# Tiles in multiples of 256 bytes and a later norm factor in a two-layer decoder trunk

## The chip, the cores and the metric

The kernel runs on one core of a Trainium2 chip. The metric is the device time of one execution in microseconds (us). Each core has a matrix engine (TensorE, "PE" in the profile; its loading of the stationary operand is "PEld"), a vector engine (DVE), a scalar engine (ACT), GpSimd (POOL) and SyncE (SP), which here only issues transfers. The engines run side by side, each through its own queue of instructions in order; 16 DMA engines move data between HBM and SBUF, the on-chip memory of 128 partitions. PE accumulates into PSUM banks.

## The reference

The input `x` is 256 tokens by 2,048 features (S = 256, D = 2048). Two layers follow each other, each with a mixer and a gated MLP, both behind an RMS norm and added to the residual stream.

```python
for l in range(DEPTH):
    h = rms_norm(x, mix_norm[l])
    h = mixer_ab(h, ...) if l % 2 == 0 else mixer_c(h, ...)
    x = x + h
    h = rms_norm(x, ffn_norm[l])
    x = x + conv_ffn(h, ffn_w_up[l], ffn_conv_w[l], ffn_conv_b[l], ffn_w_down[l])

def rms_norm(x, gain):
    return x * rsqrt(mean(x * x, axis=-1) + eps) * gain

def conv_ffn(h, w_up, conv_w, conv_b, w_down):
    z = h @ w_up                      # 2048 -> 2 * 5632
    z = causal width-3 convolution over tokens of z, + conv_b
    a, b = split(z, 2)
    return (silu(a) * b) @ w_down     # 5632 -> 2048
```

Mixer AB (layer 0) is a chunked gMLP with 8 heads beside an HGRN2 recurrence with 8 heads, both fed by one projection 2048 -> 6144, and one output projection 2048 -> 2048. Mixer C (layer 1) is attention with 16 heads, normed q and k, a forget gate and an output gate: 2048 -> 8208, and 2048 -> 2048 back. All is float32.

## The kernel before

**Arithmetic.** Every weight is streamed from HBM once, as float32, in blocks of 128 partitions x 1,024 columns (512 KB). `weights` (L142) allocates three tiles for a block: `w`, filled by a DMA on SP's queue (L150); `wh`, a rounded copy that ACT makes (L153); and `wl`, the remainder `w - wh`, by DVE (L155). Activations are split likewise: each 128-feature slice has a tile `a` (or `ya`, `yb`, `yc`, `hid`) of 512 columns, high part in 0 to 255 and low part in 256 to 511. A product is then three matmuls on PE: high x `wh`, high x `wl`, low x `wh`.

**Three forms of a projection.** `project` keeps features on partitions (L176, L179). `project_tok` (L212 to L214, and L204 for the first four slices of the kernel) has the activations stationary (128 tokens) and 512 columns of weights moving, so that tokens lie on partitions. `project_four` (L229 to L231) does the same with four 128-column pieces of the weights, and runs w_abo, w_co and all of both MLPs: 16 slices of 128 make 8 blocks of 12 matmuls for each group of 512 output columns. Its result, tokens on partitions, goes back to features on partitions in `transposed`: 32x32 transposes on DVE (L237) and 16 DMAs of 32 KB, by turns on SP's and POOL's queue (L242).

**Norm.** The projections run on `x * gain`, not normed. Squares are summed slice by slice into `acc` (ACT L314, DVE L315). `finish_tok` (L322) lets PE sum `acc` over partitions with `ones` (L326), yields once, and `rsq` (L279) makes `Rt`, one factor per token, by Ln and Exp on ACT (L99) and steps on DVE. In the MLP `four` (L771) reads `norm.Rt` right behind its `project_four` and scales the result by it as it leaves PSUM.

**Order.** The program is traced in the order of the Python code. Work beside the matmuls lies in generators: `queue` holds those not begun, `flight` those running; `tick` (L121), called before every block of weights, fills `flight` up to `depth[0]` and advances each one by a step. `LAG` = 4 ticks is the time a generator leaves for transposing DMAs. A scheduler of the framework then orders each engine's queue by the dependencies and the traced order.

**Memory.** Pools give every tag a fixed place in each partition, tag after tag, so the size of a tile sets where the tiles behind it begin. Small tiles (factors, sums) are 16 floats = 64 bytes wide (`LANE` = 16), and `pp`, the table of per-feature constants, 816 floats. The main weight pool `wp` (4 buffers of `w`, 3 each of `wh` and `wl`) exists throughout; the MLPs have a second one, `fw`, with 2 of each, which `weights` uses for every second block from turn 7 of the MLP on:

```python
if deep["pool"] is not None and deep["turn"] > 6 and deep["turn"] % 2:
    pool, nw, ns = deep["pool"], 2, 2
else:
    pool, nw, ns = wp, 4, 3
```

`fw` and the MLP's own pool `fp` lie where the mixer's tiles lay, so the first transfers into them wait until the mixer's last tiles have been read: those are read by `add_four`'s rest (L359), which adds w_co's or w_abo's result to x and feeds the next norm.

**Start.** SP issues the first weights (L81), `pp`, and further weights; ACT issues five transfers of x (L83), then loads a table of activation functions (L131); PE runs 11 small matmuls on `ones` (L134; 22 rows in the trace) while the data arrive.

Of the kernel before, what the change touches and what calls it, by code (L numbers as in the profile page):

```python
# [8 lines left out]
F32 = mybir.dt.float32  # L9
# [16 lines left out]
LAG = 4  # L26
EPS = 1e-6
WARM = 11
FETCH = {4: (8,), 8: (12,)}
LANE = 16  # L30
# [19 lines left out]
def tile_trunk(ctx: ExitStack, tc: tile.TileContext, x, pp_d, cst_d, mlev_d, msk_d,  # L50
# [80 lines left out]
    SC.preload_act_table_set(LNEXP)  # L131
# [10 lines left out]
    def weights(src, n, rows=None, w=None):  # L142
        deep["turn"] += 1
        if deep["pool"] is not None and deep["turn"] > 6 and deep["turn"] % 2:
            pool, nw, ns = deep["pool"], 2, 2
        else:
            pool, nw, ns = wp, 4, 3
        if w is None:
            w = pool.tile([P, n], F32, tag="w", name=nm("w"), bufs=nw)
            deep["dma"] = nc.sync.dma_start(  # L150
                w if rows is None else w.rearrange("p (m c) -> p m c", m=rows), src)
        wh = pool.tile([P, n], F32R, tag="wh", name=nm("wh"), bufs=ns)
        SC.activation(wh, w, AF.Copy)  # L153
# [64 lines left out]
    def project_four(w4, acts, n, k0=0):  # L218
        ps = [pm.tile([P, 512], F32, tag="pm", name=nm("pm")) for _ in range(2)]
        for k in range(0, n, 2):  # L220
# [3 lines left out]
            for T in range(2):  # L224
                for i in range(2):
# [5 lines left out]
                    PE.matmul(ps[T], al, h, start=False, stop=k + i == n - 1)  # L231
# [47 lines left out]
    def rsq(dst, src, n):  # L279
        tag = "sq" if dst.shape[-1] == S else f"rm{len(dst.shape)}{dst.shape[-1]}"  # L280
# [14 lines left out]
    class Norm:  # L295
# [26 lines left out]
        def finish_tok(self):  # L322
            p2 = bank()
            for T in range(2):
                lhs = self.acc[:, T * P:(T + 1) * P] if not self.turn else view(self.acc, T, (2, P))
                PE.matmul(p2[:, 2 * T:2 * T + 2], lhs, ones[:, 0:2], start=True, stop=True)  # L326
            Rt = cp.tile([P, LANE], F32, tag="Rt", name=nm("Rt"), bufs=2)[:, 0:2]
            yield
# [20 lines left out]
    def add_four(q, ps, z, tmp, dst, nxt):  # L349
# [4 lines left out]
        def rest():  # L354
# [8 lines left out]
            if q == 3:  # L363
                yield
                yield from nxt.finish_tok()
# [4 lines left out]
    def mixer_ab(norm):  # L370
# [40 lines left out]
        SC.dma_start(wt[:, 0], spw_d)  # L411
        SC.dma_start(wt[:, 1], spb_d.partition_broadcast(P))
        SC.dma_start(pp[:, C_CW:NPP], pp_d[:, C_CW:NPP])
        msk = hp.tile([P, NL * P], BF16, tag="msk", name="msk")
        kst = hp.tile([P, NL * P], F32, tag="smk", name="kst", bufs=1)
        SC.dma_start(kst, msk_d)
# [4 lines left out]
        ss = hp.tile([P, 4 * NH], F32, tag="ss", name="ss")  # L421
# [37 lines left out]
        gm = hp.tile([P, 4 * NH], F32, tag="gm", name="gm")  # L459
        mx, sm_, lb, omlb = (gm[:, i * NH:(i + 1) * NH] for i in range(4))  # L460
        ge = hp.tile([P, 4 * NH], F32, tag="ge", name="ge")[:, 0:3 * NH]
# [32 lines left out]
        def hgrn(h):  # L494
# [14 lines left out]
            tot = l  # L509
            for li in reversed(range(NL)):  # L510
# [468 lines left out]
```

## Time and profile before

| what | value |
|---|---|
| median of 3 runs | 2356.82 us (2355.55 to 2357.02) |
| the profiled execution: its time, its span | 2357.62 us, 2355.8 us |
| mean granted PE clock | 0.997 |
| PE, PEld, DVE, ACT, POOL busy | 2340.0, 1931.0, 1583.3, 1291.8, 260.1 us |
| HBM read, mean rate | 435.24 MB, 186 GB/s |
| L229 to L231: on `a`, on `hid` | 3 x 1408, 3 x 688 matmuls |
| L212 to L214 | 3 x 504 matmuls |
| PE idle longest | 1.5 us for wh, 1.3 us for w, 1.2 us for wl, twice 1.0 us for acc |

The table is read so: the span goes from the first to the last instruction on the core, and the time of the execution has 1.8 us around it. A busy time is the sum of an engine's instructions with overlaps counted once; two matmuls that follow each other overlap (one takes 0.39 us from start to end, the next starts 0.23 us behind it), so the distance of their starts, not their duration, is what one costs. Behind a bracket in an answer on groups stand the busy time, the mean duration in ns, and the idle time of the engine ahead of the group. In a timeline the columns are start, duration, engine, line, operation, what is written and read, and in square brackets the idle time before it and what ended it. The clock is the share of full speed that the throttle granted to PE.

### The profile page before, as it was taken

The numbers are of one execution on the slowest core, as the hardware profiler recorded it, in microseconds if no ns is written. First come the engines' busy times: TensorE is split into PE (matmuls) and PEld (weight loads), VectorE is DVE, ScalarE is ACT, GpSimd is POOL, SyncE is SP. The second block draws the span as 40 slices with busy tenths as digits, with TensorE's granted clock in tenths as the row PEclk, the third lists the DMA queues.
The fourth block names the chain that finished last, engine by engine and source line by source line (L and its number), as shares of the span: only waits on it lengthen the run. The fifth ranks groups of instructions, "written<-read, shape, count | busy, mean of one in ns | idle before, by whom it ended". The sixth has DMA issues, their size and how long they took to land.

```text
span 2355.8 us, 31594 instructions
## 1 busy us (share of the span) xinstructions
PE 2340.0 (99%) x10776; PEld 1931.0 (82%) x10776; DVE 1583.3 (67%) x2470; ACT 1291.8 (55%) x1955; POOL 260.1 (11%) x484
## 2 busy tenths in 40 slices
PE   9999999999999999999999999999999999999999
PEld 7888888788888888888788888887888888888887
DVE  7777877666566656766866666766666466557666
ACT  7655665555455545654554455555555455455542
POOL 0000002122012002111100000012121022012102
PEclk9999999999999999999999999999999999999999
DMA  8655567776666767765665555667777667667765
GB/s 269 183 166 153 150 206 219 227 213 204 209 205 198 221 193 205 222 214 177 210 191 180 172 162 165 191 201 226 220 212 216 190 210 214 200 201 215 215 204 166
DMA packets 433009, 470.94 MB, mean 200 GB/s; under 512 B 90688, under 2 KB 394064, under 8 KB 432720
## 3 DMA queue, kind: packets, MB, share of 16 engines
q1 hardware_dynamic: 415904, 449.96, 62.3%
q0 software_dynamic: 15360, 15.76, 3.1%
q10 hardware_dynamic: 1584, 3.21, 0.4%
q8 instruction: 84, 1.38, 0.3%
q14 instruction: 77, 0.63, 0.1%
HBM read 435.24 MB, written 2.11 MB: 186 GB/s over the span
## 4 chain that ended last, share of the span: by engine, by line
PE 95%; DMA 1%; DVE 1%; SPq 1%; issue 1%; ACT 0%; POOL 0%; DVEq 0%; ACTq 0%; POOLq 0%
PE pm L230 22%; PE pm L231 22%; PE pm L229 22%; PE pm L176 8%; PE pm L213 5%; PE pm L214 5%; PE pm L212 5%; PE pm L179 4%; SPq L242 1%; PE px L532 1%; DMA w<-in_w_up 0%; DMA x<-in_x 0%; PE px L713 0%; ACT wh L153 0%; PE px L677 0%
## 5 line engine op out<-in xcount | busy, mean ns | idle before, releaser
L155 DVE TENSOR_TENSOR wl<-w,wh 128x1024 fp32r<-128x1024 f32 (+1 forms) x820 | 998.7, 1221 | 663.0 <-ACT wh L153 655.9
L153 ACT ACTIVATE wh<-w 128x1024 fp32r<-128x1024 f32 (+1 forms) x820 | 864.5, 1056 | 832.7 <-PE pm L231 555.9
L229 PE MATMUL pm<-wh,a 128*128 128x512 f32 x1408 | 553.4, 393 | 2.8 <-ACT wh L153 1.5
L230 PE MATMUL pm<-wl,a 128*128 128x512 f32 x1408 | 553.9, 393 | 0.6 <-DVE wl L155 0.5
L231 PE MATMUL pm<-wh,a 128*128 128x512 f32 x1408 | 554.2, 394 | 0.0
L242 POOL DMA_DIRECT2D zt<-tmp x416 | 225.1, 549 | 1237.3 <-DVE tmp L237 1150.5
L229 PEld LDWEIGHTS pm<-wh,a 128*128 128x128 f32 x1408 | 265.1, 188 | 62.8 <-ACT wh L153 3.0
L230 PEld LDWEIGHTS pm<-wl,a 128*128 128x128 f32 x1408 | 265.4, 188 | 62.2 <-DVE wl L155 1.7
L231 PEld LDWEIGHTS pm<-wh,a 128*128 128x128 f32 x1408 | 265.2, 188 | 59.8
L231 PE MATMUL pm<-wh,hid 128*128 128x512 f32 x688 | 270.0, 392 | 0.0
L230 PE MATMUL pm<-wl,hid 128*128 128x512 f32 x688 | 269.7, 392 | 0.0
L229 PE MATMUL pm<-wh,hid 128*128 128x512 f32 x688 | 269.7, 392 | 0.0
L176 PE MATMUL pm<-a,wh 128*128 128x512 f32 x784 | 251.0, 400 | 0.0
L212 PE MATMUL pm<-wh,a 128*128 128x512 f32 x504 | 200.1, 398 | 0.3 <-ACT wh L153 0.3
L213 PE MATMUL pm<-wl,a 128*128 128x512 f32 x504 | 197.4, 392 | 2.2 <-DVE wl L155 2.2
L214 PE MATMUL pm<-wh,a 128*128 128x512 f32 x504 | 197.0, 391 | 0.0
L179 PEld LDWEIGHTS pm<-a,wl 128*128 128x128 f32 x784 | 147.3, 188 | 34.2
L179 PE MATMUL pm<-a,wl 128*128 128x256 f32 x784 | 155.1, 279 | 0.0
L230 PEld LDWEIGHTS pm<-wl,hid 128*128 128x128 f32 x688 | 129.1, 188 | 29.4
L229 PEld LDWEIGHTS pm<-wh,hid 128*128 128x128 f32 x688 | 129.2, 188 | 29.1
L231 PEld LDWEIGHTS pm<-wh,hid 128*128 128x128 f32 x688 | 129.1, 188 | 29.2
L176 PEld LDWEIGHTS pm<-a,wh 128*128 128x128 f32 x784 | 120.5, 189 | 0.4
(217 smaller groups left out, 2163.5 us busy)
## 6 DMA issues: line engine op xcount, KB each, us to landing
w<-in_w_up SPq DMA_DIRECT2D x352, 512.0 KB, 4.5
w<-in_w_dn SPq DMA_DIRECT2D x176, 512.0 KB, 4.3
w<-in_w_cqkv SPq DMA_DIRECT2D x96, 512.0 KB, 3.8
w<-in_w_abo SPq DMA_DIRECT2D x32, 512.0 KB, 4.5
w<-in_w_cg SPq DMA_DIRECT2D x32, 512.0 KB, 4.4
w<-in_w_co SPq DMA_DIRECT2D x32, 512.0 KB, 4.3
zt<-tmp SPq DMA_DIRECT2D x416, 32.0 KB, 2.5
zt<-tmp POOLq DMA_DIRECT2D x416, 32.0 KB, 2.4
```

The source lines that it names most:

```text
L153: SC.activation(wh, w, AF.Copy)
L155: V.tensor_tensor(wl, w, wh.bitcast(F32), ALU.subtract)
L176: PE.matmul(ps, wh[:, k * P:(k + 1) * P], acts[done + k], start=done + k == 0, stop=False, skip_group_check=True)
L179: PE.matmul(ps[:, S:2 * S], wl[:, k * P:(k + 1) * P], acts[done + k][:, 0:S], start=False, stop=done + k == nk - 1, skip_group_check=True)
L212: PE.matmul(ps[T], ah, h, start=k + i == 0, stop=False)
L213: PE.matmul(ps[T], ah, l, start=False, stop=False)
L214: PE.matmul(ps[T], al, h, start=False, stop=k + i == KT - 1)
L229: PE.matmul(ps[T], ah, h, start=k + i == 0, stop=False)
L230: PE.matmul(ps[T], ah, l, start=False, stop=False)
L231: PE.matmul(ps[T], al, h, start=False, stop=k + i == n - 1)
L242: (nc.sync, nc.gpsimd)[(a + b) % 2].dma_start(dst[BLK * b:BLK * (b + 1), :, a * n:(a + 1) * n], tmp[BLK * a:BLK * (a + 1), b * 4 * n:(b + ...
L532: PE.matmul(sps[:, (li - c0) * P:(li - c0 + 1) * P], E[:, li, 0], E[:, li, 1], start=True, stop=True)
```

## The change

It has four parts.

1. **Sizes.** `LANE` goes from 16 to 64, so small tiles are 256 bytes wide; `ss`, `gm`, `ct` and the tile for `rsq` become 64 floats wide, `ge` moves into `gm`, and HGRN's running products share one tile `tots`. Every SBUF tile is then a multiple of 256 bytes.
2. **The MLPs' norm factor.** `finish_tok` yields twice between L342 (L326 before) and `rsq`, is reached `WAIT` = 4 ticks later, and its matmul is ordered behind the latest matmul of `project_four`. `four` no longer scales its result at once: it returns a generator, `empty`, that yields until `norm.Rt` exists, then moves the result out of PSUM, transposes it, and waits `LAG` ticks; `start` takes a step of it at once and puts it into `flight`. `z` has 2 buffers instead of 3, and the second weight pool serves from turn 13 on.
3. **Mixer C.** The projections of q and k of the first four heads both come before the drain and the norm's end; the projection of the forget gate (`forget`) comes behind them.
4. **Start.** `pp` and the first slice of x are issued by ACT, the next four by POOL, the weights by SP. The first four slices' weights come in tiles of 1,024 columns, loaded and split in halves. The early table load at L131 is left out, 9 warming matmuls replace 11, x from slice 8 on is issued behind another block of weights, and the squares as well as the late constants are ordered behind the ACT copy of turn 5.

The diff, cut to its core:

```diff
@@ -24,10 +24,11 @@
 LAG = 4
+WAIT = 4
 EPS = 1e-6
-WARM = 11
-FETCH = {4: (8,), 8: (12,)}
-LANE = 16
+WARM = 9
+FETCH = {6: (8,), 8: (12,)}
+LANE = 64
 LEVELS = (64, 32, 16, 8, 4, 2, 1)
@@ -77,11 +78,9 @@
-    first = wp.tile([P, 512], F32, tag="w", name=nm("w"), bufs=4)
-    nc.sync.dma_start(first, w_v[0, :, 0:512])
-    for t, c0, n in xload[:5]:
-        SC.dma_start(t, x[:, c0:c0 + n, :])
-    nc.sync.dma_start(pp[:, 0:C_FFN], pp_d[:, 0:C_FFN])
+    SC.dma_start(pp[:, 0:C_FFN], pp_d[:, 0:C_FFN])
+    for i, (t, c0, n) in enumerate(xload[:5]):
+        (nc.gpsimd if i else SC).dma_start(t, x[:, c0:c0 + n, :])
     V.memset(ones, 1.0)
@@ -128,7 +127,11 @@
-    SC.preload_act_table_set(LNEXP)
+    def start(g):
+
+        if next(g, g) is not g:
+            flight.append(g)
+
     warm = pm.tile([P, 512], F32, tag="pm", name="warm")
@@ -139,20 +142,27 @@
-    def weights(src, n, rows=None, w=None):
+    def weights(src, n, rows=None, single=None):
...
-        if deep["pool"] is not None and deep["turn"] > 6 and deep["turn"] % 2:
+        if deep["pool"] is not None and deep["turn"] > 12 and deep["turn"] % 2:
...
-        if w is None:
-            w = pool.tile([P, n], F32, tag="w", name=nm("w"), bufs=nw)
+        w = pool.tile([P, n], F32, tag="w", name=nm("w"), bufs=nw)
+        wh = pool.tile([P, n], F32R, tag="wh", name=nm("wh"), bufs=ns)
+        wl = pool.tile([P, n], F32R, tag="wl", name=nm("wl"), bufs=ns)
+        parts = [slice(i, i + n // 2) for i in (0, n // 2)] if single else [slice(0, n)]
+        for p in parts:
...
-                w if rows is None else w.rearrange("p (m c) -> p m c", m=rows), src)
-        wh = pool.tile([P, n], F32R, tag="wh", name=nm("wh"), bufs=ns)
-        SC.activation(wh, w, AF.Copy)
-        wl = pool.tile([P, n], F32R, tag="wl", name=nm("wl"), bufs=ns)
-        V.tensor_tensor(wl, w, wh.bitcast(F32), ALU.subtract)
+                w[:, p] if rows is None else w.rearrange("p (m c) -> p m c", m=rows), src[:, p] if single else src)
+        for i, p in enumerate(parts):
+            if single:
+                norm, k = single
+                norm.feed_split(k + i, SC if k + i else V)
+            deep["act"] = SC.activation(wh[:, p], w[:, p], AF.Copy)
+            if deep["turn"] == 5:
+                deep["hold"] = deep["act"]
+            V.tensor_tensor(wl[:, p], w[:, p], wh[:, p].bitcast(F32), ALU.subtract)
@@ -184,24 +194,27 @@
-        for c in ((1, 1, 1, 1) + (2,) * 6 if feed else (2,) * 8):
+        for c in (2,) * 8:
...
-                for i in range(c):
-                    norm.feed_split(k + i, V if k == 0 else SC)
+                if k >= 4:
+                    for i in range(c):
+                        norm.feed_split(k + i)
...
-            wh, wl = weights(wsrc[:, k * 512:(k + c) * 512], c * 512, w=first if feed and k == 0 else None)
+            wh, wl = weights(wsrc[:, k * 512:(k + c) * 512], c * 512, single=(norm, k) if feed and k < 4 else None)
...
-            if feed and c == 1:
-                a = norm.a[k]
-                for j, (o, t) in enumerate(((0, wh), (S, wh), (0, wl))):
-                    for T in range(2):
-                        PE.matmul(ps[T], a[:, o + T * P:o + (T + 1) * P], t, start=k + j == 0, stop=False)
+            if feed and k < 4:
+                for i in range(c):
+                    a = norm.a[k + i]
+                    for j, (o, t) in enumerate(((0, wh), (S, wh), (0, wl))):
+                        for T in range(2):
+                            PE.matmul(ps[T], a[:, o + T * P:o + (T + 1) * P], t[:, i * 512:(i + 1) * 512],
+                                      start=k + i + j == 0, stop=False)
@@ -228,7 +241,7 @@
                     PE.matmul(ps[T], ah, l, start=False, stop=False)
-                    PE.matmul(ps[T], al, h, start=False, stop=k + i == n - 1)
+                    deep['mm'] = PE.matmul(ps[T], al, h, start=False, stop=k + i == n - 1)
         return ps
@@ -277,7 +290,7 @@
     def rsq(dst, src, n):
-        tag = "sq" if dst.shape[-1] == S else f"rm{len(dst.shape)}{dst.shape[-1]}"
+        tag = "sq" if dst.shape[-1] == S else "rm"
         cols = dst.shape[-1] if dst.shape[-1] == S else LANE // math.prod(dst.shape[1:-1])
@@ -308,10 +321,13 @@
             if self.n == 0:
-                SC.activation(self.acc, xT[k], AF.Square)
+                r = SC.activation(self.acc, xT[k], AF.Square)
             else:
                 sq = tp.tile([P, S], F32, tag="sq", name=nm("sq"))
-                SC.activation(sq, xT[k], AF.Square)
+                r = SC.activation(sq, xT[k], AF.Square)
+            if "mm" not in deep:
+                tc.add_manual_dep(r.ins, deep["hold"].ins.name, order, reason="not before")
+            if self.n:
                 (eng or V).tensor_tensor(self.acc, self.acc, sq, ALU.add)
@@ -323,8 +339,11 @@
                 lhs = self.acc[:, T * P:(T + 1) * P] if not self.turn else view(self.acc, T, (2, P))
-                PE.matmul(p2[:, 2 * T:2 * T + 2], lhs, ones[:, 0:2], start=True, stop=True)
+                r = PE.matmul(p2[:, 2 * T:2 * T + 2], lhs, ones[:, 0:2], start=True, stop=True)
+                if "mm" in deep:
+                    tc.add_manual_dep(r.ins, deep["mm"].ins.name, order, reason="not before")
             Rt = cp.tile([P, LANE], F32, tag="Rt", name=nm("Rt"), bufs=2)[:, 0:2]
+            yield
             yield
@@ -405,20 +425,24 @@
-        SC.dma_start(cst, cst_d)
-        SC.dma_start(pp[:, C_FFN:C_CW], pp_d[:, C_FFN:C_CW])
+        def fetch_late(*args):
+            r = SC.dma_start(*args)
+            tc.add_manual_dep(r.ins, deep["hold"].ins.name, order, reason="queue order")
+
+        fetch_late(cst, cst_d)
...
@@ -507,6 +531,7 @@
             tot = l
+            tots = hp.tile([P, S], F32, tag="tot", name=nm("tot"), bufs=1)
             for li in reversed(range(NL)):
@@ -518,7 +543,7 @@
                     V.tensor_tensor(odd, odd, view(tot, m, (-m, 2), (2, m // 2), (0, n)), ALU.mult)
-                    nt = hp.tile([P, max(m, LANE)], F32, tag=f"tot{n}", name=nm("tot"), bufs=1)[:, 0:m]
+                    nt = tots[:, S - 2 * m:S - m]
                     V.tensor_tensor(nt, view(tot, 0, (2, m)), view(tot, 1, (2, m)), ALU.mult)
@@ -637,7 +662,7 @@
         A = norm.a
-        early = project_tok(w_cqkv[0], norm)
+        early = project_tok(w_cqkv[0], norm), project_tok(w_cqkv[CH // 4], norm)
         drain()
@@ -648,26 +673,28 @@
-        f = project_norm(w_cf, A, R, hp.tile([P, S], F32, tag="f", name="f"))
...
-        nc.sync.dma_start(cb, cd.partition_broadcast(P))
+        ct = hp.tile([P, 2, 2 * CH], F32, tag="ct", name="ct")[..., 0:CH]
+
+        def forget():
+            f = project_norm(w_cf, A, R, hp.tile([P, S], F32, tag="f", name="f"))
+            fa = hp.tile([P, S], F32, tag="fa", name="fa")
...
+            V.tensor_tensor_scan(fc, on, f, 0.0, ALU.mult, ALU.add)
+            cd = dp.tile([CH, S], F32, tag="cd", name="cd")
+            nc.sync.dma_start(cd, fc[0:CH, :])
+            for T in range(2):
+                ps = bank()
+                PE.transpose(ps[:, 0:P], fc[:, T * P:(T + 1) * P], ident)
+                V.tensor_copy(ct[:, T], ps[:, 0:CH])
+            nc.sync.dma_start(cb, cd.partition_broadcast(P))
@@ -716,9 +743,11 @@
             qkv = []
-            ss = hp.tile([P, 2, 2, 4], F32, tag="ss", name=nm("ss"), bufs=2)
+            ss = hp.tile([P, 2, 2, LANE // 4], F32, tag="ss", name=nm("ss"), bufs=2)[..., 0:4]
             for j in range(3):
-                ps = early if g + j == 0 else project_tok(w_cqkv[j * (CH // 4) + g], norm)
+                if g == 0 and j == 2:
+                    forget()
+                ps = early[j] if g == 0 and j < 2 else project_tok(w_cqkv[j * (CH // 4) + g], norm)
                 z = hp.tile([P, 2, 512], F32, tag=f"z{j}", name=nm("z"), bufs=2)
@@ -770,13 +799,19 @@
             ps = project_four(w_up[l, j0:j0 + 4], A, KT)
-            Rt = norm.Rt
             tmp, zt = room()
-            z = [hp.tile([P, 512], F32, tag="z", name=nm("z"), bufs=3) for _ in range(2)]
-            for T in range(2):
-                SC.activation(z[T], ps[T], AF.Copy, scale=Rt[:, T:T + 1])
-            transposed(lambda T: z[T], tmp, zt)
-            return zt
+
+            def empty():
+                while norm.Rt is None:
+                    yield
+                z = [hp.tile([P, 512], F32, tag="z", name=nm("z"), bufs=2) for _ in range(2)]
+                for T in range(2):
+                    SC.activation(z[T], ps[T], AF.Copy, scale=norm.Rt[:, T:T + 1])
+                transposed(lambda T: z[T], tmp, zt)
+                for _ in range(LAG):
+                    yield
+
+            return zt, empty()
@@ -791,24 +826,22 @@
         def up(j0):
-            za = four(j0)
+            za, ea = four(j0)
             ca = []
...
             def gate():
-                for _ in range(LAG):
-                    yield
+                yield from ea
                 for i in range(4):
...
-            queue.append(gate())
-            zb = four(HT + j0)
+            start(gate())
+            zb, eb = four(HT + j0)
             def fill():
-                for _ in range(LAG):
-                    yield
+                yield from eb
                 for i in range(4):
```

More of the change, by code (lines that the diff above doesn't have):

```diff
@@ L363, in rest @@
             if q == 3:
-                yield
+                for _ in range(WAIT):
+                    yield
                 yield from nxt.finish_tok()
@@ L419, in mixer_ab @@
                         .to_broadcast([P, NH, P]), ALU.mult)
-        ss = hp.tile([P, 4 * NH], F32, tag="ss", name="ss")
+        ss = hp.tile([P, LANE], F32, tag="ss", name="ss")
         for g in range(2):
@@ L458, in mixer_ab @@
         gam = pp[:, C_GAM:C_GAM + 3 * NH]
-        gm = hp.tile([P, 4 * NH], F32, tag="gm", name="gm")
+        gm = hp.tile([P, LANE], F32, tag="gm", name="gm")
         mx, sm_, lb, omlb = (gm[:, i * NH:(i + 1) * NH] for i in range(4))
-        ge = hp.tile([P, 4 * NH], F32, tag="ge", name="ge")[:, 0:3 * NH]
+        ge = gm[:, 4 * NH:7 * NH]
         g3 = [gam[:, i * NH:(i + 1) * NH] for i in range(3)]
@@ L649, in mixer_c @@
         V.tensor_scalar(gq, pp[:, C_QN:C_QN + 1], float(P) ** -0.5, None, ALU.mult)
[L651 to L670 removed]
+        ct = hp.tile([P, 2, 2 * CH], F32, tag="ct", name="ct")[..., 0:CH]
+        cb = hp.tile([P, CH, S], F32, tag="cb", name="cb")
+        def forget():
+            f = project_norm(w_cf, A, R, hp.tile([P, S], F32, tag="f", name="f"))
+            fa = hp.tile([P, S], F32, tag="fa", name="fa")
+            fc = hp.tile([P, S], F32, tag="fc", name="fc")
+            on = hp.tile([P, S], F32, tag="on", name="on")
+            V.memset(on, 1.0)
+            V.tensor_scalar(f, f, pp[:, C_BF:C_BF + 1], None, ALU.add)
+            SC.activation(fa, f, AF.Abs)
+            act(fa, fa, AF.Exp, scale=-1.0)
+            act(fa, fa, AF.Ln, bias=one1)
+            V.scalar_tensor_tensor(f, f, 0.0, fa, ALU.min, ALU.subtract)
+            V.tensor_tensor_scan(fc, on, f, 0.0, ALU.mult, ALU.add)
[6 more added lines that the diff above has]
+            nc.sync.dma_start(cb, cd.partition_broadcast(P))
         def attend(h, q, k, v):
@@ L772, in four @@
             ps = project_four(w_up[l, j0:j0 + 4], A, KT)
-            Rt = norm.Rt
             tmp, zt = room()
-            z = [hp.tile([P, 512], F32, tag="z", name=nm("z"), bufs=3) for _ in range(2)]
-            for T in range(2):
-                SC.activation(z[T], ps[T], AF.Copy, scale=Rt[:, T:T + 1])
-            transposed(lambda T: z[T], tmp, zt)
-            return zt
+            def empty():
[6 more added lines that the diff above has]
+                for _ in range(LAG):
+                    yield
+            return zt, empty()
         def conv(z, j, half):
@@ L818, in fill @@
                     yield
-            queue.append(fill())
+            start(fill())
         y = hp.tile([P, 2, D], F32, tag="y", name=nm("y"))
@@ L839, in rest @@
                 if q == 3 and not last:
-                    yield
+                    for _ in range(WAIT):
+                        yield
                     yield from nxt.finish_tok()
```

26 lines of the change are left out of this document (5 added, 21 removed).

## The prediction

> **What bounds the kernel now.** I read the page first: PE's share, and the chain that ended last.
>
> ```profile
> PE 2340.0 (99%) x10776; PEld 1931.0 (82%) x10776; DVE 1583.3 (67%) x2470; ACT 1291.8 (55%) x1955; POOL 260.1 (11%) x484
> PE 95%; DMA 1%; DVE 1%; SPq 1%; issue 1%; ACT 0%; POOL 0%; DVEq 0%; ACTq 0%; POOLq 0%
> ```
>
> PE is the bound. Time can be saved in two ways only: PE idles less, or its matmuls follow one another faster. So the next view is the groups of PE instructions, one answer for each stage: w_abo (310 to 390 us), the first FFN (840 to 1080 us), w_co (1528 to 1622 us). All are 128x512 matmuls of the same types.
>
> ```profile
> L230 PE MATMUL pm<-wl,yb 128*128 128x512 f32 x63 | 24.5, 389 | 0.0
> L230 PE MATMUL pm<-wl,a 128*128 128x512 f32 x256 | 100.4, 392 | 0.0
> L230 PE MATMUL pm<-wl,yc 128*128 128x512 f32 x126 | 49.7, 395 | 0.0
> ```
>
> Nothing is waited for (0.0), yet the mean is 389, 392 and 395 ns. These durations overlap; what costs is the distance of starts. In the timeline of PE, w_abo first, then w_co:
>
> ```profile
> 349.64 0.39 PE L229 MATMUL pm<-wh,ya 128*128 128x512 f32 x1
> 351.91 0.39 PE L230 MATMUL pm<-wl,ya 128*128 128x512 f32 x1
> ...
> 1559.79 0.39 PE L230 MATMUL pm<-wl,yc 128*128 128x512 f32 x1
> 1562.12 0.40 PE L231 MATMUL pm<-wh,yc 128*128 128x512 f32 x1
> ```
>
> Each pair is ten matmuls apart: 2.27 us and 2.33 us. Averaged over whole stages the distance is 226.7 ns in w_abo, 230.2 in the FFNs, 232.4 in w_co. Last, the timeline of PE where the norm factor is made, in layer 0 and in layer 1, and the table of stretches behind it (columns: PE, PEld, DVE, ACT, POOL, clock, DMA share, GB/s):
>
> ```profile
> 411.97 0.39 PE L231 MATMUL pm<-wh,a 128*128 128x512 f32 x1
> 413.35 0.63 PE L326 MATMUL px<-ones,acc 128*128 128x2 f32 x4 [0.99 <-DVE acc L315]
> 415.52 1.22 PE L229 MATMUL pm<-wh,a 128*128 128x512 f32 x2 [1.53 <-ACT wh L153]
> ...
> 1632.82 0.63 PE L326 MATMUL px<-ones,acc 128*128 128x2 f32 x4 [1.00 <-DVE acc L315]
> 1634.71 0.73 PE L229 MATMUL pm<-wh,a 128*128 128x512 f32 x2 [1.26 <-DMA w<-in_w_up]
> ```
>
> ```profile
> 414.70:421.50 6.80, 5.95 (x13) 4.26 (x14) 3.47 (x6) 3.40 (x5) 0.00 (x0) 0.50 0.97 330
> 1636.70:1640.00 3.30, 3.30 (x10) 2.55 (x9) 1.23 (x1) 0.66 (x1) 0.00 (x0) 0.50 0.96 317
> ```
>
> PE waits for the sum of squares (L326), then for weights; after each gap the granted clock is 0.50 for 6.8 and 3.4 us.
>
> **Part 1: tiles at multiples of 256 bytes.** The three distances go with where the operands begin in a partition. By the sizes in the code, the main weight pool and the `a` tiles begin at multiples of 256 bytes; `hid`, the second FFN weight pool and `yc` begin 128 past one, because the small tiles are 64 bytes (LANE 16). With moving and stationary operand at the same remainder: w_abo 226.7, FFN 227.9. With different ones: FFN 232.6 (2,992 of 6,007 undisturbed starts), w_co 232.4. In the changed kernel every tile is a multiple of 256 bytes, so all share one remainder (128). Gain if the effect is the address: FFN 3 x (1,408 + 688) = 6,288 matmuls x (230.2 - 226.7) = 22.0 us; w_co 3 x 128 x (232.4 - 226.7) = 2.2 us; together 24.2. Not all goes: the FFN's equal pairs stand at 227.9, above 226.7, because 254 L231 whose weights and activations begin at certain equal remainders of 2,048 bytes are at 232.4, and the matmuls behind them at 230.8. The layout as built has about as many (2.2 to 2.7 us), so 24.2 - 2.5 = 21.7, and I take 21.5. Lower end: all FFN and w_co matmuls end at 227.9: 6,288 x 2.3 + 384 x 4.5 = 16.2. Upper end: 24.2. Project_tok's L212 to L214 are at 226.7 in w_cqkv and L176/L179 have equal remainders before and after: nothing from them.
>
> [...]
>
> **Part 2: the norm factor later.** Before, L326 stands in PE's queue behind six of the eight blocks (12 matmuls, 2.7 us each) of the first w_up group; PE and everything behind it wait until DVE has added the last square (413.13 us). Of PE's starts in 412 to 421 us, 6.0 us are above the usual distance: 1.15 before L326, 1.76 behind it, the rest from clock 0.50. In 1,631 to 1,640 us it is 4.75. The second wait has its own cause: the weights of block 7 sit in the second pool, whose DMA was issued only at 410.19, after the reuse of memory that L359's adds still read, and landed at 414.07. The change takes both: the second pool is used only after turn 12, so blocks 7, 9 and 11 go to the main pool, and L326 (now L342) follows about block 9, the first of the second group. Due there near 420 us, it finds the squares, done at 413.3. What is late next: activation `a` 15 is ready near 413.0 and needed near 414.8; with main pool buffers free as in before, the weights for blocks 7 and 8 are issued at 402.7 and 403.3, land by 409.6, and are needed from 412. PSUM: the first group's two banks are now kept until the factor is known, near block 11; the third group needs them at block 17, some 5 blocks (14 us) later. The evacuation, transposes, their 16 DMAs on SP and POOL and the conv steps come later for the first group only; ACT (44.5 of 80 us busy in w_abo, 370 of 690 in FFN) and DVE (448 of 690) can take them. The four small matmuls remain (0.25 us). Gain 10.75 - 0.25 = 10.5; lower end 9 (a wait of 1.5 us left at one layer), upper 10.75.
>
> **Part 3: the start.** Before, ACT issues five x loads (0.75 to 4.62), loads a table (4.66 to 5.94), and makes the first wh at 5.95, so the first real matmul starts at 6.63; further waits at 12.0, 13.0 and 16.6 cost 0.46, 0.69, 0.62. After, ACT issues two (2.3 us), the one table load left is earlier, and w, which landed at 4.12, lets wh start at once; x0 landed at 4.27, and its split takes 0.5. First matmul near 5.3: a gain of 1.3. But from 2 to 18 us DMA is at 0.90 to 1.02 of its capacity and the bytes are the same, so the waits at 12 and 13 may take half back; the last (0.62), with weights issued earlier, I expect gone. POOL's queue now carries x1 to x6 (0.55 us an issue by L242): x1 landed at 4.91 before; 1 us later would cover its own slack. The nine pairs of warming matmuls end near 4.8 instead of 5.7. Gain 1.2, ends 0 and 2.
>
> [...]
>
> **Small edits.** q and k ahead of w_cf in mixer_c: the wait of L667 for the scan (0.59) and L213's at 1137 us (1.37) remain, since as many matmuls stand between; cb's 2 MB (8.9 us) land near 1199, needed near 1206. The merged `tots` orders L522 slightly differently among the L502 and L532 matmuls: -0.7 to +0.7, taken as 0; z with 2 buffers instead of 3: 0, as at most two are alive. ACT has 8 instructions fewer, PE none. The tail after the last matmul (2,350.2 to 2,355.8) is unchanged.
>
> **Sum.** The profiled execution took 2,357.6, 0.8 above the median of 2,356.8. 2,357.6 - 21.5 - 10.5 - 1.2 = 2,324.4; less 0.8 on the median's footing: 2,324 us (-1.4%). Ends added up: 2,356.8 - 16.2 - 9 - 0 = 2,331.6, and 2,356.8 - 24.2 - 10.75 - 2 = 2,319.8; 0.7 for `tots` widens both. A measurement of this kernel tells about 0.2% (4.7 us) from no change.
>
> **Rivals.**
> - *The stalls only move* (10%). L342, or block 7 or 8, waits for something else in the denser queue, and the clock falls to 0.50 again, as it did after gaps of under 3 us. For it: DMA share 0.97 around the stall. Against it: the slacks above. Only parts 1 and 3: 2,356.8 - 22.7 = 2,334.
> - *Addresses do nothing* (8%). Something else in w_co and FFN sets 232 ns, for example the reading of four 128-wide pieces by `view`. Against it: w_abo reads in the same way at 226.7, and the FFN's two classes alternate within a stage. Then 2,356.8 - 11.7 = 2,345.
> - *Slower: equal addresses collide* (5%). 254 equal pairs at 232.4 show that some equal placements are slow. If the new layout makes nearly all pairs such, 7,056 matmuls of the fours rise from a mean of 230.1 to 232.4 (+16), 1,512 of L212 to L214 from 226.7 (+8.6), less 11.7: 2,370. It decides from a share of (24.2 + 11.7) / (8,568 x 5.7 ns) = 74% of the pairs on. Against it: the FFN already has 1,056 pairs at (128, 128), at 227.9.
>
> **How the numbers follow.** 75% for the forecast, 10, 8 and 5 for the rivals, 2 for a mixture that ends within 0.2%. Faster 0.93, same 0.02, slower 0.05. The range 2,316 to 2,336 holds forecast and first rival; the other two are left out.
>
> **What would show it.** Part 1: L229 to L231 on `a`, `hid` and `yc` at a mean near 389 to 390 ns, like `ya`. Part 2: no wait for acc at L342, no stretch at clock 0.50 near 412 and 1,610. Part 3: first L212-type matmul near 5.3. It is wrong if `yc` stays at 395, if PE waits for w or `a` late in the first w_up group, or if `a` matmuls of project_tok rise above 389.

## The result and the profile after

The changed kernel takes 2319.62 us (median of four runs, 2319.09 to 2321.23) against 2356.92 us: a ratio of 0.9844, 95% interval 0.9827 to 0.9861. That is 37.3 us less; 32.8 had been forecast, and the time lies in the forecast range of 2,316 to 2,336 us. The profiled execution took 2321.2 us with a span of 2319.4, the longest of the four (the others span 2317.3 to 2317.9).

First PE's share, the chain and the groups, from the page of the changed kernel (behind the bracket: busy us, mean ns, idle before). L242 to L244 are the old L229 to L231:

```profile
PE 2309.2 (100%) x10772; PEld 1927.4 (83%) x10772; DVE 1582.2 (68%) x2470; ACT 1288.7 (56%) x1954; POOL 262.7 (11%) x488
PE 99%; DMA 0%; DVE 0%; ACT 0%; issue 0%; SPq 0%; DVEq 0%
L243 PE MATMUL pm<-wl,a 128*128 128x512 f32 x1408 | 547.7, 389 | 0.0
L243 PE MATMUL pm<-wl,hid 128*128 128x512 f32 x688 | 267.6, 389 | 0.0
```

All of the fours' matmuls now have the 389 ns that only `ya` and `yb` had. The same in the stage of w_co (1510 to 1590 us), where it was 395:

```profile
L243 PE MATMUL pm<-wl,yc 128*128 128x512 f32 x118 | 45.9, 389 | 0.0
```

The norm's sum in PE's timeline, layer 0; it has no wait in front of it, and the clock stays at 1.00 (table of stretches, columns PE, clock, DMA share, GB/s):

```profile
418.78 0.39 PE L244 MATMUL pm<-wh,a 128*128 128x512 f32 x1
419.01 0.52 PE L342 MATMUL px<-ones,acc 128*128 128x2 f32 x4
419.39 0.48 PE L242 MATMUL pm<-wh,a 128*128 128x512 f32 x1
```

```profile
410.00:421.00 11.00, 11.00 (x52) 1.00 0.97 320
1610.00:1625.00 15.00, 15.00 (x69) 1.00 0.95 304
```

What is left of PE's waits is small and new in part (behind the colon: us in total, times, longest; L735 are the attention's transposes):

```profile
PE px L735 <- DVE sc L730: 1.5, 2, 1.3
PE pm L216 <- ACT wh L162: 1.0, 1, 1.0
PE pm L226 <- DVE wl L165: 0.8, 1, 0.8
```

Where the time went, by the starts of PE's matmuls at the ends of the stages in both timelines:

| stretch | before, us | after, us | difference |
|---|---|---|---|
| start to the 300th matmul | 74.01 | 73.60 | -0.41 |
| from there to w_abo (gMLP, HGRN) | 234.80 | 233.86 | -0.94 |
| w_abo | 86.84 | 86.84 | 0.00 |
| first MLP | 735.65 | 718.57 | -17.08 |
| mixer C up to w_co | 394.80 | 395.35 | +0.55 |
| w_co | 89.00 | 86.85 | -2.15 |
| second MLP | 735.12 | 719.01 | -16.11 |
| behind the last matmul's start | 5.61 | 5.37 | -0.24 |

They add up to the 36.4 us between the two spans. "The fours" are the matmuls of `project_four`. Each undisturbed distance from one start to the next in them, sorted by whether its moving and its stationary operand begin at the same remainder of 256 bytes (equal) or not:

| | equal | unequal | equal, but the first behind an unequal one |
|---|---|---|---|
| before | 3,335 at 227.45 ns | 3,426 at 232.62 | 266 at 231.62 |
| after | 7,050 at 226.68 ns | none | none |

Against the 226.68 ns of after, these are 3,426 x 5.94 + 266 x 4.94 + 3,335 x 0.77 ns = 24.2 us: two thirds of the gain.

### The profile page after: what moved, and what is told of

Same layout as the page of the kernel before. It is cut to its first block, busy times and chain, and to the rows that moved or that the text cites. A ratio compares the mean times of both kernels' runs of the same rounds, so it can differ in the third digit from the quotient of the medians.

```text
span 2319.4 us, 31614 instructions
## 1 busy us (share of the span) xinstructions
PE 2309.2 (100%) x10772; PEld 1927.4 (83%) x10772; DVE 1582.2 (68%) x2470; ACT 1288.7 (56%) x1954; POOL 262.7 (11%) x488
## 3 DMA queue, kind: packets, MB, share of 16 engines
q1 hardware_dynamic: 415760, 449.94, 63.4%
## 4 chain that ended last, share of the span: by engine, by line
PE 99%; DMA 0%; DVE 0%; ACT 0%; issue 0%; SPq 0%; DVEq 0%
PE pm L242 23%; PE pm L244 23%; PE pm L243 23%; PE pm L186 8%; PE pm L226 5%; PE pm L227 5%; PE pm L225 5%; PE pm L189 4%; PE px L557 1%; DMA w<-in_w_v 0%; PE px L740 0%; PE px L704 0%; PE px L711 0%; PE px L735 0%; PE px L526 0%; PE px L710 0%
## 5 line engine op out<-in xcount | busy, mean ns | idle before, releaser
L162 ACT ACTIVATE wh<-w 128x1024 fp32r<-128x1024 f32 (+1 forms) x820 | 863.3, 1056 | 809.5 <-PE pm L244 525.8
L242 PE MATMUL pm<-wh,a 128*128 128x512 f32 x1408 | 547.9, 389 | 0.0
L244 PE MATMUL pm<-wh,a 128*128 128x512 f32 x1408 | 547.7, 389 | 0.0
L244 PEld LDWEIGHTS pm<-wh,a 128*128 128x128 f32 x1408 | 264.3, 188 | 54.9
L242 PEld LDWEIGHTS pm<-wh,a 128*128 128x128 f32 x1408 | 264.3, 188 | 54.8
L242 PE MATMUL pm<-wh,hid 128*128 128x512 f32 x688 | 267.6, 389 | 0.0
L244 PE MATMUL pm<-wh,hid 128*128 128x512 f32 x688 | 267.6, 389 | 0.0
L186 PE MATMUL pm<-a,wh 128*128 128x512 f32 x784 | 250.9, 400 | 0.0
L189 PEld LDWEIGHTS pm<-a,wl 128*128 128x128 f32 x784 | 147.3, 188 | 34.1
L189 PE MATMUL pm<-a,wl 128*128 128x256 f32 x784 | 155.2, 279 | 0.0
L244 PEld LDWEIGHTS pm<-wh,hid 128*128 128x128 f32 x688 | 129.2, 188 | 26.8
L242 PEld LDWEIGHTS pm<-wh,hid 128*128 128x128 f32 x688 | 129.2, 188 | 26.7
L186 PEld LDWEIGHTS pm<-a,wh 128*128 128x128 f32 x784 | 120.5, 189 | 0.4
```

What stands on the lines that cost most here:

```text
L162: deep["act"] = SC.activation(wh[:, p], w[:, p], AF.Copy)
L186: PE.matmul(ps, wh[:, k * P:(k + 1) * P], acts[done + k], start=done + k == 0, stop=False, skip_group_check=True)
L189: PE.matmul(ps[:, S:2 * S], wl[:, k * P:(k + 1) * P], acts[done + k][:, 0:S], start=False, stop=done + k == nk - 1, skip_group_check=True)
L242: PE.matmul(ps[T], ah, h, start=k + i == 0, stop=False)
L244: deep['mm'] = PE.matmul(ps[T], al, h, start=False, stop=k + i == n - 1)
```

## Experiments on part 1: the place of the operands

**The sizes alone, on the kernel before.** `ss`, `gm`, `ge` and `ct` are widened as in the change; `z` has 2 buffers so that the memory suffices.

```diff
-LANE = 16
+LANE = 64
-        tag = ... else f"rm{len(dst.shape)}{dst.shape[-1]}"
+        tag = ... else "rm"
...
+            tots = hp.tile([P, S], F32, tag="tot", ...)
...
-            z = [hp.tile([P, 512], F32, tag="z", name=nm("z"), bufs=3) for _ in range(2)]
+            z = [hp.tile([P, 512], F32, tag="z", name=nm("z"), bufs=2) for _ in range(2)]
```

> The kernel before with the sizes alone: LANE 64, the widened small tiles, tots, and z with 2 buffers so that the memory suffices. Address theory: 24 us less than before (the fours at 226.7 to 227), so about 2333; both waits for the norm and the half clock at 412 and 1631 us stay (10.8 us). Rival, addresses do nothing: 2357 within 2, yc at 395 ns as before. If the gain needed the later norm as well, it would lie between.

Measured: 2332.89 us against 2356.81, ratio 0.9897 (0.9882 to 0.9912): 23.9 less. All starts in the fours are 226.68 ns apart on average; the waits for the norm are there as before (PE waits twice 1.0 us for `acc`, then 1.4 and 1.2 us for weights, and the clock is at 0.50 for 3.4 us behind each). From its page:

```profile
L230 PE MATMUL pm<-wl,hid 128*128 128x512 f32 x688 | 267.6, 389 | 0.0
L229 PE MATMUL pm<-wh,a 128*128 128x512 f32 x1408 | 548.1, 390 | 2.6 <-ACT wh L153 1.4
```

So the sizes bring their gain without the later norm. The stretch with HGRN (from the 300th matmul to w_abo) is 233.84 here, as in the changed kernel: its 0.9 us came with this part too, though the runs do not separate the merged `tots` from the alignment.

**The activations moved by 128, 64 and 32 bytes, on the changed kernel.** A pad ahead of the pool of `a` moves every stationary activation against the main weight pool; the second weight pool moves along with them. The diff is that for 128 bytes, where `one1` is smaller as well, which puts the main weight pool at a multiple of 256. For 64 and 32 bytes the pad has 16 and 8 floats, and `one1` stays.

```diff
+    apool.tile([P, 32], F32, tag="pad", name="pad", bufs=1)
...
-    one1 = cp.tile([P, LANE], F32, tag="one1", name="one1")[:, 0:1]
+    one1 = cp.tile([P, 32], F32, tag="one1", name="one1")[:, 0:1]
```

> The changed kernel with all stationary activations moved by 128 bytes against the main weight pool (a pad ahead of the pool of a, one1 128 bytes smaller); the second weight pool moves with the activations. Unequal are then 4,056 of 7,056 matmuls of the fours, all 1,536 of project_tok, and project. Address theory: fours 4,056 x 5.8 ns = 23.5 us more, project_tok 1,536 x 5.8 = 8.9 more if it is sensitive as well, so 2343 to 2352, and up to 2357 if project pays too. Rival, addresses do nothing: 2320 within 2.

> As the shift by 128 bytes, but by 64. If what counts is the same place within 256 bytes, the cost is like that of 128: 2343 to 2357. If only the two halves of 256 bytes matter (places 128 apart), 2320. If the cost grows with the distance, about half: 2331 to 2338.

> As the shift by 64 bytes, but by 32. Same place within 256 bytes: 2343 to 2357. Same place within 32 bytes, or a multiple of it, is enough: 2320. A cost that grows with the distance: about a quarter, 2326 to 2329.

| | time, us | to before (95%) | fours equal, ns | fours unequal | project_tok |
|---|---|---|---|---|---|
| changed kernel | 2319.62 | 0.9844 (0.9827 to 0.9861) | 226.68 | - | 227.55 |
| by 128 | 2354.09 | 0.9986 (0.9977 to 0.9996) | 227.58 | 4,050 at 232.57 | 232.63 |
| by 64 | 2357.30 | 1.0002 (0.9992 to 1.0011) | 228.58 | 4,050 at 233.33 | 233.32 |
| by 32 | 2359.80 | 1.0012 (1.0003 to 1.0022) | 228.55 | 4,050 at 233.48 | 233.15 |

A pad of 32 bytes undoes the gain of the whole change. The cost does not grow with the distance, and neither 64 nor 32 bytes are without it; of the places tried, only the same one within 256 bytes is free (226.68 ns). From the kernel moved by 32 bytes, w_co, w_abo and project_tok (1,530 to 1,620 us, 310 to 390, 1,230 to 1,260):

```profile
L244 PE MATMUL pm<-wl,yc 128*128 128x512 f32 x125 | 49.4, 395 | 0.0
L244 PE MATMUL pm<-wl,yb 128*128 128x512 f32 x64 | 25.3, 395 | 0.0
L228 PE MATMUL pm<-wh,a 128*128 128x512 f32 x38 | 15.0, 395 | 0.0
```

w_abo and project_tok, fast in before and in the changed kernel (there 389 ns), are as slow here as w_co was before (395 ns), with no wait shown. The rows add up to within a microsecond: for 64 bytes 4,050 x 6.65 (fours, unequal) + 2,750 x 1.90 (fours, equal) + 1,440 x 5.8 ns (project_tok), less 0.2 for the first equal ones behind unequal ones and less 2.05 in `project` (below), is 38.3 us; measured are 2357.30 - 2319.62 = 37.7.

In the same three kernels, the equal pairs in between are slower too (227.6 to 228.6 instead of 226.7). In before that had looked like a rule of its own on 2,048 bytes; where all pairs are equal it is gone. The starts show which pairs these are. In the MLPs blocks of 12 matmuls from the main pool and from the second pool follow each other by turns. In before, behind an unequal block, the first three starts of an equal one are 231.7, 232.5 and 230.8 ns apart (means over some 250 blocks), and the other nine 226.7 to 226.8. With the activations moved by 128 bytes it is again the first three; moved by 64 or 32 bytes it is the first five (225.8 to 235.8), and from the sixth on 226.7. So an unequal block slows the start of the equal block behind it; what carries over is not shown.

`project` is the exception: the mean distance of L186 (feature-major, more than 700 pairs) is 233.0 ns with all places equal, and 231.3, 229.4 and 229.2 when moved by 128, 64 and 32. Its L189 goes from 116.3 to 118.2, 117.0 and 119.0. Equal places are not best for it; the net is at most 2 us.

**All tiles at a multiple of 256 instead of 128 past one.**

```diff
-    one1 = cp.tile([P, LANE], F32, tag="one1", name="one1")[:, 0:1]
+    one1 = cp.tile([P, 32], F32, tag="one1", name="one1")[:, 0:1]
```

> The changed kernel with one1 128 bytes smaller, so that every tile behind it begins at a multiple of 256 bytes instead of 128 past one. If only the place of the operands relative to each other counts: the fours again at 226.7 ns, 2320 within 1.5. If the remainder 128 itself were good, the fours rise above 227.5, 2326 or more. [...]

Measured: 2319.58 us, fours 226.67 ns. So it is the place of the operands relative to each other, not the remainder. As for the loads into these tiles, the 300th matmul comes at 72.81 us instead of 73.60, but four other kernels with the changed layout and start have it at 73.30 to 74.36. The share of the DMA engines' time in the main queue:

```profile
q1 hardware_dynamic: 415760, 449.94, 63.4%
```

that of the changed kernel, and at multiples of 256:

```profile
q1 hardware_dynamic: 415760, 449.94, 62.7%
```

That is 1.2% less of the engines' time for the same bytes, but in one profiled execution of each. In the kernel moved by 128 bytes the main pool begins at a multiple of 256 too, and there the share is 62.6% of 2352.4 us, 1,473 us; in the changed kernel it is 63.4% of 2319.4 us, 1,470 us. These runs do not settle whether loads into tiles at a multiple of 256 bytes take less of the engines' time, and the time of the kernel (2319.58 against 2319.62 us) shows nothing of it.

## Experiments on part 2: the two edits of the norm

**The second pool from turn 7 again, on the changed kernel.**

```diff
-        if deep["pool"] is not None and deep["turn"] > 12 and deep["turn"] % 2:
+        if deep["pool"] is not None and deep["turn"] > 6 and deep["turn"] % 2:
```

> The changed kernel, but the second weight pool serves from turn 7 again. If the late weights of block 7 are a cause of their own, they return without the wait for the sum: a gap of some 3 us at block 7 in both layers and perhaps clock 0.50 behind it, 6 to 11 us more, 2326 to 2331. If the second wait was only a follower of the first (weights held back because PE stood at the sum), 2320 within 1.5.

Measured: 2331.03 us (2329.86 to 2333.59), 11.4 more. With the sum out of the way, PE still stops after block 6, for about as long as before, now for the weights alone (timeline of PE, both layers):

```profile
410.56 0.39 PE L244 MATMUL pm<-wh,a 128*128 128x512 f32 x1
413.69 1.03 PE L242 MATMUL pm<-wh,a 128*128 128x512 f32 x2 [2.73 <-ACT wh L162]
...
1614.19 0.39 PE L244 MATMUL pm<-wh,a 128*128 128x512 f32 x1
1617.81 0.73 PE L242 MATMUL pm<-wh,a 128*128 128x512 f32 x2 [3.24 <-ACT wh L162]
```

and the clock falls behind it, to 0.50 for 3.4 us in each layer (table of stretches, whose clock is the mean of the stretch):

```profile
413.60:421.00 7.40, 7.08 (x24) 0.77 0.92 293
1617.80:1620.00 2.20, 1.66 (x4) 0.74 1.06 360
```

**The norm where it was, on the changed kernel.** `four` scales and transposes its result at once, not in `empty`.

```diff
-WAIT = 4
+WAIT = 1
-                if "mm" in deep:
-                    tc.add_manual_dep(r.ins, deep["mm"].ins.name, order, reason="not before")
...
-            yield
+            Rt = norm.Rt
+            z = [hp.tile([P, 512], F32, tag="z", name=nm("z"), bufs=2) for _ in range(2)]
...
-                while norm.Rt is None:
-                    yield
...
```

> The changed kernel, but with the norm's sum where it was before (one yield, WAIT 1, no order behind the fours' last matmul, results scaled at once); the second pool still from turn 13 on. The wait for acc alone returns: 1.15 us in each layer, 2.3 together, 2322, if a gap so short leaves the clock alone; 3.4 and 1.7 us more if the clock falls as before, 2327. If the sum's place is the whole cause, all 10.8: 2330.

Measured: 2321.08 us (2320.01 to 2321.60), 1.5 more; the two MLPs together take 1.1 us more in the profiled execution. The sum stands near 412.8 and 1612.4, now one matmul into block 7, with 0.25 us of gap in front and 0.35 in the four small matmuls (timeline of PE):

```profile
412.30 0.39 PE L242 MATMUL pm<-wh,a 128*128 128x512 f32 x1
412.77 0.63 PE L342 MATMUL px<-ones,acc 128*128 128x2 f32 x4
413.27 0.48 PE L243 MATMUL pm<-wl,a 128*128 128x512 f32 x1
```

**One number changed in the kernel before.**

```diff
-        if deep["pool"] is not None and deep["turn"] > 6 and deep["turn"] % 2:
+        if deep["pool"] is not None and deep["turn"] > 12 and deep["turn"] % 2:
```

> The kernel before with one number changed: the second weight pool from turn 13 on. If the late weights are the whole of part 2, 10 us less than before, 2347, with no clock 0.50 near 412 and 1631 us, and the wait for acc under 0.5 us. If the wait for the sum stays by itself: 2.3 us of gaps remain, 2349, and with a lower clock behind them up to 2352.

Measured: 2347.03 us against 2356.88, ratio 0.9959 (0.9945 to 0.9973): 9.9 less. Its timeline and stretches around the sum:

```profile
412.67 0.39 PE L229 MATMUL pm<-wh,a 128*128 128x512 f32 x1
413.26 0.63 PE L326 MATMUL px<-ones,acc 128*128 128x2 f32 x4 [0.21 <-DVE acc L315]
413.76 0.48 PE L230 MATMUL pm<-wl,a 128*128 128x512 f32 x1
```

```profile
412.00:421.00 9.00, 8.79 (x41) 1.00 0.95 312
1625.00:1640.00 15.00, 14.93 (x68) 1.00 0.81 238
```

With the second pool from turn 13 on, L326 stands one matmul behind the start of block 7, and the wait for `acc` is 0.2 us instead of 1.0. So the four combinations are:

- both old: 0;
- the pool's edit alone: -9.9 us (on before);
- the norm's edit alone: nothing that the runs can tell (2331.0; both old, with the sizes but also with the old start and the old mixer C, gave 2332.9, and the old start alone costs 2.7, below);
- both: some 1 us beyond the pool's edit alone.

The wait for the sum was not a part of its own: it lay within the time in which the weights of block 7 were missing anyway.

## Experiments on the start, the POOL queue and mixer C

**The start of before, on the changed kernel.** L81 to L84, the early table load, 11 warming matmuls and blocks of 512 columns come back.

```diff
-WARM = 9
-FETCH = {6: (8,), 8: (12,)}
+WARM = 11
+FETCH = {4: (8,), 8: (12,)}
-    for i, (t, c0, n) in enumerate(xload[:5]):
-        (nc.gpsimd if i else SC).dma_start(t, x[:, c0:c0 + n, :])
+    for t, c0, n in xload[:5]:
+        SC.dma_start(t, x[:, c0:c0 + n, :])
...
```

> The changed kernel with the start of before (L81 to L84, 11 warming matmuls, the early table load, four blocks of 512 columns, x from slice 8 behind the earlier block). My prediction's 1.2 us: 2320.8. By the traces, in which the 300th matmul comes 0.41 us earlier after the change than before: 2320.0. In either case the first real matmul at 6.6 to 7.1 instead of 5.7.

Measured: 2322.28 us (2321.93 to 2322.53), 2.7 more, above both. The 300th matmul is 0.66 us later; the rest is elsewhere, more than a thousand us behind the start (timeline of PE, lines with waits):

```profile
1120.89 0.50 PE L219 MATMUL pm<-wl,a 128*128 128x512 f32 x1 [1.29 <-DVE wl L161]
```

It is the wait that before had at 1137 us (1.37 us by the starts) and the changed kernel lost. In before:

```profile
1138.61 0.50 PE L213 MATMUL pm<-wl,a 128*128 128x512 f32 x1 [1.21 <-DVE wl L155]
```

One thing that the start hands on so far is a count: the changed start puts four loads of x on POOL's queue. That queue pauses, in the kernel before and in the changed one, at these places (timeline of POOL; x5 means five DMAs issued, in brackets the idle time before):

```profile
1112.65 1.63 POOL L242 DMA_DIRECT2D zt<-tmp  x3 [7.23 <-issue]
1116.64 2.71 POOL L242 DMA_DIRECT2D zt<-tmp  x5 [2.36 <-issue]
```

```profile
1083.24 3.80 POOL L255 DMA_DIRECT2D zt<-tmp  x7 [72.68 <-issue]
1089.12 0.55 POOL L255 DMA_DIRECT2D zt<-tmp  x1 [2.09 <-issue]
```

There are four such pauses of 2.1 to 2.5 us in the traces of all thirteen kernels, always behind the 113th, 219th, 325th and 431st DMA on POOL's queue, 106 apart, however the kernel's times move. Four of these DMAs are loads of x with the new start and none with the old one, so the first two pauses fall behind the 113th and the 219th transposing DMA with the old start and behind the 109th and the 215th with the new one. (The expectation below has smaller counts for the third and the fourth, since it leaves out the 32 DMAs that bring back w_co's result.)

In before the second pause cuts a group of eight behind its third DMA. POOL's last two of that group then come behind weight loads of 512 KB: issued at 1118.3 and 1118.8, they land at 1122.2 and 1123.9, 4 to 5 us later; the three issued just before them took 1.8. The next transpose into `tmp` has to wait for them, DVE idles (2.9 us at 1121 to 1124), its queue runs behind and `wl` of mixer C's first blocks comes too late. In the changed kernel the second pause falls behind the seventh DMA of an earlier group, and all 16 transposing DMAs of the group in question have landed by 1102.2, ahead of the weights.

**The count alone.** Four of the first group's DMAs go from POOL to SP; the start is as in the change.

```diff
+        calls[0] += 1
         for a in range(4):
             for b in range(4):
-                (nc.sync, nc.gpsimd)[(a + b) % 2].dma_start(...)
+                (nc.sync, nc.gpsimd)[(a + b) % 2 if a > 1 or calls[0] > 1 else 0].dma_start(...)
```

> The changed kernel with four of the 16 transposing DMAs of the very first group moved from POOL's queue to SP's; all else as it is. POOL's queue pauses 2.1 to 2.5 us after a fixed number of its DMAs: in before behind the 113th, 219th, 293rd and 399th transposing DMA, in the changed kernel, which has four loads of x ahead of them on that queue, behind the 109th, 215th, 289th and 395th. If that count sets the wait for wl at the start of mixer C (1.37 us at 1137 in before, none in after, 1.45 at 1119 with the old start), the pause falls after the third of a group of eight near 1096 us again and the wait returns near 1119: 1.4 us more, 2321. Rival, the start itself matters by the order it leaves: no such wait, 2319.6.

Measured: 2321.31 us (2321.07 to 2322.70), 1.7 more. The second pause is still behind the 215th of POOL's transposing DMAs, but with four fewer in the first group this one is again the third of the later group of eight, and the wait is back (timelines of POOL and of PE):

```profile
1093.88 1.63 POOL L258 DMA_DIRECT2D zt<-tmp  x3 [6.65 <-issue]
1097.87 2.71 POOL L258 DMA_DIRECT2D zt<-tmp  x5 [2.37 <-issue]
```

```profile
1119.98 0.50 PE L226 MATMUL pm<-wl,a 128*128 128x512 f32 x1 [1.39 <-DVE wl L165]
```

Five of the thirteen kernels have the second pause in that place, and four of them have the wait: before, the sizes alone, the old start, and this one; no kernel has the wait without the pause there. But the pause is not enough: the fifth, the kernel before with the one number changed, has it behind the same DMA (at 1108.4 us), but only one of POOL's DMAs then lands behind a weight load, DVE idles 1.7 us, and mixer C has no such wait. What makes the pause and what ends it was not tried.

**Mixer C in the old order, on the changed kernel.**

```diff
-        early = project_tok(w_cqkv[0], norm), project_tok(w_cqkv[CH // 4], norm)
+        early = project_tok(w_cqkv[0], norm)
...
+        forget()
-                if g == 0 and j == 2:
-                    forget()
-                ps = early[j] if g == 0 and j < 2 else project_tok(...)
+                ps = early if g + j == 0 else project_tok(...)
```

> The changed kernel with mixer C in the order of before (q, drain, forget gate, k). If the new order caused the wait of the attention's transposes for DVE (1.53 and 0.42 us near 1197 and 1217), they go: 2318. If it saved the wait for wl of 1.37 us that before had at 1137 us, that returns: 2320 to 2321. Both may cancel: 2320 within 1.

Measured: 2320.17 us (2319.53 to 2320.44): no difference that can be measured. The wait for the forget gate's scan is 0.51 at 1148 instead of 0.56 at 1169 (by the starts). The attention's transposes (L735) wait 0.3 us here. With the changed order they wait 1.5 us in the changed kernel's profile and 1.4 in that moved by 32 bytes, 0.7 in that at multiples of 256, and at most 0.2 in the others. It varies with what goes before; the new order brings nothing here.

No kernel tried is faster than the changed one by more than the measurement can tell.

## Why the prediction was right or wrong

- **Part 1, 21.5 us forecast.** The mechanism was right: 24.2 by the starts, 23.9 by the sizes alone. What was mis-sized is the term "about as many (2.2 to 2.7 us)" for slow equal pairs. They were read as pairs at certain remainders of 2,048 bytes; they are the first matmuls behind an unequal block, so they are gone with the unequal ones, the fours stand at 226.68, and the upper end, 24.2, was the value.
- **The rival "addresses do nothing"** falls: by a pad alone the mean distance of unequal pairs becomes 232.6 to 233.5 ns instead of 226.7. The runs show that it depends on where the two operands begin; why it does, and why within 256 bytes, they do not show. **"The stalls only move"** did not come: L342 has no wait, and the clock is 1.00 in both stretches.
- **The slower rival (equal places collide)** rested on the same 254 pairs and fell with them. (The pairs at (128, 128) in before are 1,032 by the built program's addresses, not 1,056; nothing hangs on it.)
- **Part 2, 10.5 us forecast.** The size was right (5.0 and 5.9 us more in the two MLPs when the pool goes back), the cause only half. "The second wait has its own cause" holds; but "PE and everything behind it wait until DVE has added the last square" was counted as time to be gained by moving L326, and moving it gains about 1 us beside the pool's edit and nothing without it. Two waits behind each other on PE had been read as two causes: with the first taken away, the second took its place whole. That the sum came out is in part luck: the change holds both edits, and the one of the pool brings nearly all of it.
- **Part 3, 1.2 us forecast:** 0.4 to 0.7 at the 300th matmul. The first real matmul came at 5.71 instead of the "near 5.3" (x0, now issued behind `pp`, landed at 5.11 instead of the 4.27 that was reckoned with, and PE waits 0.45 us for its split). Of the later waits only the last went: the third tile of x, now issued by POOL, landed at 8.74 instead of 7.60, and PE waits 0.97 us for the `wh` made behind it. So data that came later took part of the gain back, which the lower end had allowed for.
- **Small edits.** "L213's at 1137 us (1.37) remain, since as many matmuls stand between" failed: it went, by the four loads of x on POOL's queue, which had been priced only at the start. `tots` was taken as 0 within 0.7; the stretch with HGRN became 0.9 shorter, whether by `tots` or by the alignment. L735's 1.5 us in the profiled execution were not foreseen.
- **The sum.** 4.4 us short of the measured gain: 2.7 from part 1, 1.4 from the wait at 1137, 0.9 from HGRN, less 0.5 to 0.8 of the start's forecast. The rest is within the spread of the runs.

## What to carry to other kernels

When groups of equal matmuls with no waits have different means, compare where their operands begin: here small tiles of 64 instead of 256 bytes cost 24 us in matmuls that do not use these tiles. Where one engine shows two waits in a row, take away each alone before crediting either; the one that ends last may cover the other (here the pool's edit alone brought 9.9 us, the norm's alone nothing that the runs can tell). And a queue's count of transfers is a thing that a change moves as well: four loads at the start moved a pause that had cost 1.4 us more than a thousand us later.

## What had not been expected

- A pad of 32 bytes between the pools costs 40 us in 2320 (2359.80), more than the whole change gains, and the slower matmuls of w_abo, w_co and project_tok show no wait for it (0.0 us in the rows above, at 395 ns).
- POOL's queue pauses 2.1 to 2.5 us behind fixed counts of its DMAs, in all thirteen kernels: behind the 113th (four loads of x and 109 transposes, or 113 transposes), then after every 106 further.
- Gaps of 2.7 and 3.2 us on PE were followed by 3.4 us at a granted clock of 0.50 (second pool from turn 7 on the changed kernel); gaps of 1.2 to 1.4 us (the wait for `wl` in mixer C) were not, in before and in the kernel with the four DMAs moved.
